# When the first latent tiles are normalised, and where layer 1's modulation is emitted, in a two-layer diffusion trunk on one core

## The chip, the cores and the metric

The kernel runs on one core of one Trainium2 chip. Its time is the device time of one execution in microseconds (us). A core has five engines that this text names: TensorE (PE in the profile; its weight loads are PEld), VectorE (DVE), ScalarE (ACT), GpSimd (POOL) and SyncE (SP), whose queue issues the DMAs. Each engine works through its own instructions in a fixed order.

## The reference

Two layers run over 1024 latent tokens and 256 context tokens of width 1024, in float32:

```python
for i in range(DEPTH):
    sh1, sc1, g1, sh2, sc2, g2 = modulation(c, w_ada[i], b_ada[i])         # silu(c) @ w_ada + b_ada, in six parts
    csh1, csc1, cg1, csh2, csc2, cg2 = modulation(c_ctx, w_ada[i], b_ada[i])
    h = modulate(rms_norm(x, norm1_g[i]), sh1, sc1)
    hc = modulate(rms_norm(ctx, norm1_g[i]), csh1, csc1)
    a_z, bq, bk, bv, cq, ck, cv = split_proj(h @ w_in[i])                  # and the same of hc
    ...
    x = x + g1 * (jnp.concatenate([out_a, out_b, out_c], axis=-1) @ w_out[i])
    x = x + g2 * conv_ffn(modulate(rms_norm(x, norm2_g[i]), sh2, sc2), w_up[i], conv_w[i], conv_b[i], w_down[i])
    # in layer 0 the context gets the same two updates
```

out_a is a chunked spatial gating, out_b a windowed attention with 8 heads, out_c a differential attention with 4 heads. conv_ffn is an up-projection to 2 x 2816 features, a convolution of width 3 over positions, silu(gate) * val, and a down-projection.

## The kernel before

**Arithmetic.** Every float32 operand is split in two parts, hi = round(x) and lo = x - hi, and a product is three matmuls (`mm3`). A weight unit (`wunit`) is one DMA into `raw` (three buffers, by SP), a rounding copy by ScalarE (L115) and a subtraction by VectorE or GpSimd (L109); its tile is `wsp` (three buffers). TensorE needs both parts.

**Order.** The program is written for a tile framework that schedules it: it simulates a time line of its own while the program is emitted, and from it decides the order of instructions on each engine. The order in which the code emits work is thus a hint, and what stands in which order is seen only in the resulting instruction lists.

**Start of layer 0.** Tokens are taken in tiles of 128: 0 to 7 are latent, 8 and 9 are context. `load_x` brings one tile from memory into `xin` (L336), transposes it on TensorE in two groups of four (L345), copies the result to `xc` (ScalarE L349, VectorE L347) and stores it to `x_s` in memory (L350). `norm_front` makes the mean square, GpSimd's power -0.5 (`nrs`, L211), a diagonal `dg` (L213), a broadcast by a matmul (L215) and the multiplication in place (L217); `norm_back` applies scale and shift (L225, L227), rounds to `h` (L228) and subtracts. `load_norm` is load_x and norm_front. Tiles 8, 9 and 0 went through load_norm ahead of the first projection; `norms` then finished the five tiles `al` = (8, 9, 0, 1, 2), and `ipset` projected all five with column blocks 3 and 2 of w_in (`inproj`; for each tile an `mm3` of 24 matmuls, L132, into `z`).

**Attention.** Until about 1100 us the attention of layer 0 runs, between and beside projections. `attn_c` ends each unit with a small chain: a reduction (`css`), VectorE's products, GpSimd's power -0.5 (`crs`, L748), VectorE's product (L749), the scaled output `o` (L751) and a transpose on TensorE (L755), whose result goes to memory (`o_s`) and from there, with the other heads, into the output projection (`oT` by L786).

**The MLP.** It runs over three groups of tokens (G0[0], G0[1], G0[2] in layer 0). Features are taken in steps f of 128, 22 in all, in blocks of 4, 4, 4, 4, 3, 3. A step has two halves (gate and value), each a w_up unit of 128 x 1024 (two halves' L115 rows are written `wsp 128x1024`) and 24 matmuls (L130). ScalarE (L847) and VectorE (L851, L854) do the convolution; L860, L861, L862, L864 and L109 make the gated product `g` in two parts. `down` takes a block's g with eight w_down units (128 x 512) of 12 matmuls each. Because five g buffers exist, down of the first block runs after five steps, the next after four more. While a group runs, `hook(f)` is called once in each step between its two halves, and puts other work there.

**Layer 1's modulation.** It is 12 column chunks of 512 (`ch`). `mod_wide` (L147 on) makes one chunk from four quarters of w_ada: a DMA of 512 KB into `mraw` (three buffers, L160), for each of its two k-slices and each stream a ScalarE scaling by the condition (the first into the accumulator `mev`, L166; the others into `mtr`, two buffers, L169), and for each `mtr` an add on GpSimd (L170). After the fourth quarter VectorE transposes and sums (L173, L174). Chunks 0 to 3, with both streams, ran in G0[1] at f = 0, 3, 6, 9; chunks 4 to 11, with one stream, in G0[2] at f = 0 to 7, a whole chunk in each call.

Of the kernel before, what the change touches and what calls it, by code (L numbers as in the profile page):

```python
# [25 lines left out]
AD = "mmmmd"  # L26
# [26 lines left out]
def trunk(ctx: ExitStack, tc: tile.TileContext, a: dict):  # L53
# [100 lines left out]
    def mod_wide(L, ch, ns, mkraw, mkacc, mktr):  # L154


        acc = [mkacc() for _ in range(ns)]
        for j in range(4):
            raw = mkraw()
            sp.dma_start(out=raw, in_=a["w_ada"][L, j * 256:j * 256 + 256, ch * 512:ch * 512 + 512]  # L160
                         .rearrange("(k p) c -> p k c", p=P))
            for k in range(2):
                for s in range(ns):
                    c1 = cpad[:, 2 * j + k, s:s + 1]
                    if j == 0 and k == 0:
                        act.activation(out=acc[s], in_=raw[:, k], func=AF.Identity, scale=c1)  # L166
                    else:
                        pr = mktr()
                        act.activation(out=pr, in_=raw[:, k], func=AF.Identity, scale=c1)  # L169
                        pool.tensor_tensor(out=acc[s], in0=acc[s], in1=pr, op=ALU.add)  # L170
        for s in range(ns):
            tr = mktr()
            dve.transpose(tr, acc[s])  # L173
            dve.tensor_reduce(out=st["modr"][:, :, ch, :, s].rearrange("p b m -> p m b"),  # L174
                              in_=tr.rearrange("p (m b j) -> p m b j", b=4, j=32), axis=AX.X, op=ALU.add)

# [154 lines left out]

    def load_x(i, wk, mkps):

        src = a["x"][0, i * P:i * P + P, :] if i < NLT else a["ctx"][0, (i - NLT) * P:(i - NLT) * P + P, :]
        xin = wk.tile([P, D], F32, tag="xin", name="xin")
        sp.dma_start(out=xin, in_=src)  # L336
        xc = wk.tile([P, KT, P], F32, tag="xc", name="xc", bufs=3)
        sq = wk.tile([P, D], F32, tag="nb", name="nb")
# [71 lines left out]

    def inproj(L, cb, tiles, hts, wk, wx, mkz, mkps, ws_=None):
        last = L == DEPTH - 1
        ws_ = ws_ or inproj_w(L, cb, wx)
        for i in tiles:
            kvonly = last and i >= NLT
            if kvonly and cb < 2:
# [579 lines left out]
    def modwide(L, ch, ns, p):  # L996
        mod_wide(L, ch, ns, lambda: p.tile([P, 2, 512], F32, tag="mraw", name="mraw", bufs=3),
                 lambda: p.tile([P, 512], F32, tag="mev", name="mev", bufs=2),
                 lambda: p.tile([P, 512], F32, tag="mtr", name="mtr", bufs=2))
# [8 lines left out]

    def load_norm(i):
        xc, ss = load_x(i, nwk, mkT)  # L1010
        norm_front(xc, mkT, None, xc, ss)
        return xc, "done"
# [4 lines left out]
    w3 = inproj_w(0, 3, wx)  # L1017
    pre.append(load_norm(0))
    ini.release()
# [3 lines left out]

    def ipset(L, tiles, cbs, wk_=None, wx_=None, w=None):
        for cb in cbs:
            wl = inproj(L, cb, tiles, hts, wk_ or wk, wx_ or wx, mkz, mkU, w)
            w = None
        return wl

    al, be = (8, 9, 0, 1, 2), (3, 4, 5, 6, 7)  # L1030
    norms(0, al, hts, hp, nwk, mkT, pre=pre, eng=NE[0], add=AD[0])
    setup2(ini2, 0, mkU)
    ipset(0, al, (3, 2), w=w3)
    setup3(ini2, 0, mkU)
# [58 lines left out]
    def hook(f):  # L1093
        ahead(0, G0[2], X3, f, HK[1], "x3")
        if f in (0, 3, 6, 9):
            modwide(1, f // 3, 2, ini)

# [15 lines left out]
    def hook(f):  # L1113
        if f < 8:
            modwide(1, 4 + f, 1, ini)
        if f == 3:
# [126 lines left out]
```

## Time and profile before

| | |
|---|---|
| time, median of 3 runs | 3356.69 us (3352.62 to 3362.18) |
| profiled execution | 3354.95 us |
| its span | 3353.1 us |
| granted TensorE clock, mean | 0.975 |
| DMA traffic | 499.52 MB, mean 149 GB/s |
| GpSimd's adds of the modulation, L170 | 112, 175.8 us, 1583 ns each |
| ScalarE's roundings of weights, L115 | 660, 555.9 us |
| VectorE's subtractions of weights, L109 | 516, 565.9 us |

The span is the time between the first and the last instruction of the profiled execution; the execution's time has a little around it. An engine's busy time is the sum of its instructions. In a table of stages, each row is a stretch (start:end), its length, then busy time and number of instructions for TensorE, its weight loads, VectorE, ScalarE and GpSimd, the granted TensorE clock, the DMA share and GB/s. In a timeline, each row has a start, a duration, the engine, the line and what it does, and in brackets the idle time before it and what ended that. In a table of groups, the two numbers behind the first bar are busy time in us and the mean of one in ns.

### The profile page before, as it was taken

How to read it: one execution, taken by the hardware profiler on the slowest of the kernel's cores; microseconds unless marked ns; L12 is line 12 of the kernel's file. 1: busy time of each engine (PE TensorE's matmuls, PEld its weight loads, DVE VectorE, ACT ScalarE, POOL GpSimd, SP SyncE). 2: the span in 40 equal slices, each digit the busy share in tenths (PEclk: the TensorE clock that was granted, in tenths of full speed). 3: DMA queues.
4: the chain of work that ended last, by engine and by line, in shares of the span. 5: the costliest groups of instructions: out<-in, count | busy, mean ns of one | idle time of the engine just before them, and what ended most of it. 6: DMA issues, size and time to landing. Idle time of an engine off the chain costs nothing. (4 is left out here: it accounts for less than half of the span.)

```text
span 3353.1 us, 54588 instructions
## 1 busy us (share of the span) xinstructions
PE 3164.3 (94%) x19503; PEld 2753.6 (82%) x19503; DVE 2342.6 (70%) x5306; ACT 1744.9 (52%) x3059; POOL 883.6 (26%) x1170
## 2 busy tenths in 40 slices
PE   6999998999999899999999899999999989999999
PEld 3777556887888798989999777666887779999998
DVE  5776756756878785878677678647786685666666
ACT  3555546555555653646444345556665564454443
POOL 1545211222233550128001154222322323222000
PEclk8999999999999999999999899999999999999999
DMA  8655777344542853378243556445645446434433
GB/s 259 194 156 162 223 248 186 89 121 124 136 116 83 255 154 110 103 207 242 87 117 112 160 149 161 126 139 136 167 135 149 122 118 189 120 111 135 137 114 108
DMA packets 754127, 499.52 MB, mean 149 GB/s; under 512 B 81480, under 2 KB 697792, under 8 KB 753856
## 3 DMA queue, kind: packets, MB, share of 16 engines
q1 hardware_dynamic: 753856, 496.03, 51.7%
q8 instruction: 155, 2.54, 0.3%
q14 instruction: 116, 0.95, 0.1%
HBM read 432.48 MB, written 63.44 MB: 148 GB/s over the span
## 5 line engine op out<-in xcount | busy, mean ns | idle before, releaser
L130 PE MATMUL z<-h,wsp 128*128 128x386 f32 (+3 forms) x5280 | 871.7, 318 | 20.4 <-DVE t L854 10.2
L130 PEld LDWEIGHTS z<-h,wsp 128*128 128x128 f32 x5280 | 822.0, 190 | 36.4 <-issue 13.9
L115 ACT ACTIVATE wsp<-raw 128x1024 fp32r<-128x1024 f32 (+2 forms) x660 | 555.9, 845 | 442.1 <-PE z L130 179.0
L109 DVE TENSOR_TENSOR wsp<-raw,wsp 128x1024 fp32r<-128x1024 f32 (+2 forms) x516 | 565.9, 1099 | 121.3 <-ACT wsp L115 118.5
L130 PE MATMUL z<-g,wsp 128*128 128x386 f32 (+3 forms) x2640 | 463.5, 323 | 17.8 <-ACT wsp L115 5.7
L130 PEld LDWEIGHTS z<-g,wsp 128*128 128x128 f32 x2640 | 418.1, 192 | 35.8 <-issue 11.0
L132 PE MATMUL z<-wsp,h 128*128 128x512 f32 x1584 | 404.8, 402 | 13.0 <-ACT wsp L115 3.3
L109 POOL TENSOR_TENSOR wsp<-raw,wsp 128x128 fp32r<-128x128 f32 x528 | 253.9, 513 | 448.8 <-ACT wsp L115 397.2
L132 PEld LDWEIGHTS z<-wsp,h 128*128 128x128 f32 x1584 | 291.6, 191 | 79.9 <-ACT wsp L115 4.3
L130 PE MATMUL zS<-h,wsp 128*128 128x386 f32 (+1 forms) x2112 | 333.7, 313 | 8.1 <-DVE t L854 3.2
L130 PEld LDWEIGHTS zS<-h,wsp 128*128 128x128 f32 x2112 | 318.9, 190 | 10.9 <-ACT wsp L115 4.3
L847 ACT ACTIVATE t<-z,cw 128x386 f32<-128x386 f32 (+3 forms) x220 | 137.8, 627 | 209.8 <-PE z L130 208.6
L851 DVE SCALAR_TENSOR_TENSOR t<-z,cw,t 128x255 f32<-128x255 f32 (+3 forms) x264 | 132.5, 502 | 144.6 <-ACT t L847 144.2
L682 ACT ACTIVATE ec<-ec,nmc 128x1280 f32<-128x1280 f32 (+1 forms) x144 | 182.1, 1265 | 52.1 <-DVE ec L483 51.0
L170 POOL TENSOR_TENSOR mev<-mev,mtr 128x512 f32<-128x512 f32 x112 | 175.8, 1583 | 124.6 <-ACT mtr L169 121.7
L130 PE MATMUL z<-oT,wsp 128*128 128x384 f32 (+2 forms) x1056 | 200.0, 336 | 4.9 <-DMA oT<-o_s 3.4
L130 PE MATMUL zS<-g,wsp 128*128 128x386 f32 (+1 forms) x1056 | 184.4, 319 | 14.9 <-ACT wsp L115 4.3
L483 DVE TENSOR_SCALAR_CACHE_REDUCE ec<-S,nmc 128x512 f32<-128x512 f32 (+1 forms) x256 | 156.7, 612 | 56.0 <-PE S L679 52.7
L879 DVE SCALAR_TENSOR_TENSOR xg<-z,mods,xg 128x384 f32<-128x384 f32 (+5 forms) x288 | 140.4, 501 | 75.8 <-PE z L130 74.7
L130 PEld LDWEIGHTS z<-oT,wsp 128*128 128x128 f32 x1056 | 176.1, 188 | 15.1 <-issue 4.9
L370 POOL TENSOR_TENSOR rs<-ss,cst 128x8 f32<-128x8 f32 (+1 forms) x76 | 119.5, 1572 | 259.5 <-DVE ss L368 187.7
L579 POOL TENSOR_SCALAR dgb<-cst,ls 128x128 f32<-128x128 f32 x144 | 89.2, 632 | 372.7 <-PE T L616 182.3
(248 smaller groups left out, 4848.1 us busy)
## 6 DMA issues: line engine op xcount, KB each, us to landing
raw<-in_w_up_dram SPq DMA_DIRECT2D x264, 512.0 KB
mraw<-in_w_ada_dram SPq DMA_DIRECT2D x96, 512.0 KB
raw<-in_w_down_dram SPq DMA_DIRECT2D x192, 256.0 KB
Kc<-qk_s SPq DMA_DIRECT2D x96, 320.0 KB
raw<-in_w_in_dram SPq DMA_DIRECT2D x52, 512.0 KB
raw<-in_w_out_dram SPq DMA_DIRECT2D x48, 512.0 KB
raw<-in_w_down_dram SPq DMA_DIRECT2D x104, 192.0 KB
qk_s<-st SPq DMA_DIRECT2D x18, 512.0 KB
```

What stands on the lines that cost most here:

```text
L109: eng.tensor_tensor(out=lo, in0=src, in1=hi.bitcast(F32), op=ALU.subtract)
L115: act.activation(out=hl[:, 0], in_=raw, func=AF.Copy)
L130: pe.matmul(ps, w(i, k), h(j, k), start=s, stop=e)
L132: pe.matmul(ps, h(i, k), w(j, k), start=s, stop=e)
L170: pool.tensor_tensor(out=acc[s], in0=acc[s], in1=pr, op=ALU.add)
L370: pool.tensor_tensor(out=rs[:, :ns], in0=ss[:, 1, :ns], in1=mhalf[:, :ns], op=ALU.pow)
L483: dve.tensor_scalar(out=neg, in0=s_ap, scalar1=-1.0, scalar2=init, op0=ALU.mult, op1=ALU.min, accum_out=acc)
L579: pool.tensor_scalar(out=dgs[ti][:, j], in0=ident, scalar1=ls[:, j:j + 1], scalar2=None, op0=ALU.mult)
L682: act.activation(out=e[:, :nk], in_=e[:, :nk], func=AF.Exp, scale=-1.0, bias=acc, accum_out=l1[:, m, ti:ti + 1])
L847: act.activation(out=t[:, o:o + n], in_=ps[:, :n], func=AF.Identity, scale=cw[:, L, 1, ft:ft + 1], bias=cw[:, L, 3, ft:ft + 1])
L851: dve.scalar_tensor_tensor(out=t[:, o + b + 1:o + e], in0=ps[:, b:e - 1], scalar=cw[:, L, 0, ft:ft + 1], in1=t[:, o + b + 1:o + e], op0=AL ...
L879: dve.scalar_tensor_tensor(out=xs, in0=ps[:, b + o0:b + o1], scalar=mods[:, L, 40 + ct, s:s + 1], in1=xs, op0=ALU.mult, op1=ALU.add)
```

## The change

It has two parts. In the first, tiles 0 and 1 are only fetched ahead of the first projection (`fetch_x`), norms finishes tiles 8 and 9, and a function `between` is called before each tile is projected with column block 3: it loads and normalises the tile that stands two places further in `al`. Column block 2 follows in a call of its own. In the second, `mod_wide` returns a function `quarter(j)`. In G0[1], one quarter is emitted in each of the steps 0 to 15; in G0[2], the 32 quarters are emitted over steps 0 to 13, two or three in each. The number of instructions on each engine stays the same.

```diff
--- before.py
+++ after.py
@@ -155,7 +155,8 @@
 
 
         acc = [mkacc() for _ in range(ns)]
-        for j in range(4):
+
+        def quarter(j):
             raw = mkraw()
             sp.dma_start(out=raw, in_=a["w_ada"][L, j * 256:j * 256 + 256, ch * 512:ch * 512 + 512]
                          .rearrange("(k p) c -> p k c", p=P))
@@ -168,11 +169,15 @@
                         pr = mktr()
                         act.activation(out=pr, in_=raw[:, k], func=AF.Identity, scale=c1)
                         pool.tensor_tensor(out=acc[s], in0=acc[s], in1=pr, op=ALU.add)
-        for s in range(ns):
-            tr = mktr()
-            dve.transpose(tr, acc[s])
-            dve.tensor_reduce(out=st["modr"][:, :, ch, :, s].rearrange("p b m -> p m b"),
-                              in_=tr.rearrange("p (m b j) -> p m b j", b=4, j=32), axis=AX.X, op=ALU.add)
+            if j < 3:
+                return
+            for s in range(ns):
+                tr = mktr()
+                dve.transpose(tr, acc[s])
+                dve.tensor_reduce(out=st["modr"][:, :, ch, :, s].rearrange("p b m -> p m b"),
+                                  in_=tr.rearrange("p (m b j) -> p m b j", b=4, j=32), axis=AX.X, op=ALU.add)
+
+        return quarter
 
     def mod_sum(L, c0, c1, ns, mkps):
 
@@ -329,11 +334,15 @@
         dve.tensor_scalar(out=cw[:, L, :, NFF:], in0=cw[:, L, :, NFF:], scalar1=0.5, scalar2=None, op0=ALU.mult)
 
 
-    def load_x(i, wk, mkps):
-
+    def fetch_x(i, wk):
         src = a["x"][0, i * P:i * P + P, :] if i < NLT else a["ctx"][0, (i - NLT) * P:(i - NLT) * P + P, :]
         xin = wk.tile([P, D], F32, tag="xin", name="xin")
         sp.dma_start(out=xin, in_=src)
+        return xin
+
+    def load_x(i, wk, mkps, xin=None):
+
+        xin = fetch_x(i, wk) if xin is None else xin
         xc = wk.tile([P, KT, P], F32, tag="xc", name="xc", bufs=3)
         sq = wk.tile([P, D], F32, tag="nb", name="nb")
         ss = sm.tile([P, 1], F32, tag="xss", name="xss")
@@ -408,10 +417,12 @@
         return [wunit(a["w_in"][L, u * 256:u * 256 + 256, cb * 512:cb * 512 + 512], 2, 512, wx if u == 3 else ws,
                       eng=E_[WD[st["wd"]][u]]) for u in range(4)]
 
-    def inproj(L, cb, tiles, hts, wk, wx, mkz, mkps, ws_=None):
+    def inproj(L, cb, tiles, hts, wk, wx, mkz, mkps, ws_=None, between=None):
         last = L == DEPTH - 1
         ws_ = ws_ or inproj_w(L, cb, wx)
         for i in tiles:
+            if between:
+                between(i)
             kvonly = last and i >= NLT
             if kvonly and cb < 2:
                 continue
@@ -994,7 +1005,7 @@
     setup_c(ini, mkU)
 
     def modwide(L, ch, ns, p):
-        mod_wide(L, ch, ns, lambda: p.tile([P, 2, 512], F32, tag="mraw", name="mraw", bufs=3),
+        return mod_wide(L, ch, ns, lambda: p.tile([P, 2, 512], F32, tag="mraw", name="mraw", bufs=3),
                  lambda: p.tile([P, 512], F32, tag="mev", name="mev", bufs=2),
                  lambda: p.tile([P, 512], F32, tag="mtr", name="mtr", bufs=2))
 
@@ -1006,8 +1017,8 @@
     modset(0, (2,), ini, "mev", ini, "mraw", 16, mkz, mkU)
     setup(ini, mkU)
 
-    def load_norm(i):
-        xc, ss = load_x(i, nwk, mkT)
+    def load_norm(i, xin=None):
+        xc, ss = load_x(i, nwk, mkT, xin)
         norm_front(xc, mkT, None, xc, ss)
         return xc, "done"
 
@@ -1015,22 +1026,31 @@
     modset(0, (3, 0, 1), ini, "mev", ini, "mraw", 16, mkz, mkU)
     mod_scale(0, 0)
     w3 = inproj_w(0, 3, wx)
-    pre.append(load_norm(0))
+    xins = [fetch_x(i, nwk) for i in (0, 1)]
     ini.release()
     hp = mkpool("h0", 8, "right")
     wk = mkpool("wk0", 2, "right")
     hts = {}
 
-    def ipset(L, tiles, cbs, wk_=None, wx_=None, w=None):
+    def ipset(L, tiles, cbs, wk_=None, wx_=None, w=None, between=None):
         for cb in cbs:
-            wl = inproj(L, cb, tiles, hts, wk_ or wk, wx_ or wx, mkz, mkU, w)
+            wl = inproj(L, cb, tiles, hts, wk_ or wk, wx_ or wx, mkz, mkU, w, between)
             w = None
         return wl
 
     al, be = (8, 9, 0, 1, 2), (3, 4, 5, 6, 7)
-    norms(0, al, hts, hp, nwk, mkT, pre=pre, eng=NE[0], add=AD[0])
+    norms(0, al[:2], hts, hp, nwk, mkT, pre=pre, eng=NE[0], add=AD[0])
+
+    def between(i):
+
+        n = al.index(i) + 2
+        if n < len(al):
+            j = al[n]
+            norms(0, (j,), hts, hp, nwk, mkT, pre=[load_norm(j, xins.pop(0) if xins else None)], eng=NE[0], add=AD[0])
+
     setup2(ini2, 0, mkU)
-    ipset(0, al, (3, 2), w=w3)
+    ipset(0, al, (3,), w=w3, between=between)
+    ipset(0, al, (2,))
     setup3(ini2, 0, mkU)
     norms(0, be, hts, hp, nwk, mkT, eng=NE[1], add=AD[1])
     ini2.release()
@@ -1092,8 +1112,10 @@
 
     def hook(f):
         ahead(0, G0[2], X3, f, HK[1], "x3")
-        if f in (0, 3, 6, 9):
-            modwide(1, f // 3, 2, ini)
+        if f < 16:
+            if f % 4 == 0:
+                st["q"] = modwide(1, f // 4, 2, ini)
+            st["q"](f % 4)
 
     wide(True)
     mlp(0, G0[1], *st["x2"], M, hook)
@@ -1111,8 +1133,10 @@
     al, be = (8, 9, 0, 1), (2, 3, 4, 5, 6, 7)
 
     def hook(f):
-        if f < 8:
-            modwide(1, 4 + f, 1, ini)
+        for n in range(32 * f // 14, 32 * (f + 1) // 14 if f < 14 else 0):
+            if n % 4 == 0:
+                st["q"] = modwide(1, 4 + n // 4, 1, ini)
+            st["q"](n % 4)
         if f == 3:
             setup2(ini, 1, mkT)
             setup3(ini, 1, mkT)
```

What the scheduler makes of it is shown at three places; the number behind a name in the first of them is the buffer's.

The first place is the start of layer 0, on TensorE: the rows around the projection of tile 0 (`z_651`), before. h_439 is tile 0's, xin_420 is tile 2, dg_455 and dg_475 belong to the norms of tiles 1 and 2.

```order
L132 MATMUL z_600<-wsp_341,h_409 128x512 x5
L345 MATMUL T_426<-cst_69,xin_420 128x128 x4
L345 MATMUL T_432<-cst_69,xin_420 128x128 x4
L215 MATMUL T_457<-dg_455,cst_69 128x128
L215 MATMUL T_477<-dg_475,cst_69 128x128
L132 MATMUL z_651<-wsp_326,h_439 128x512 x2
L345 MATMUL T_1176<-cst_69,xin_1170 128x128 x4
L132 MATMUL z_651<-wsp_326,h_439 128x512 x4
```

The same place with the change, where h_461 is tile 0's, xin_611 is tile 2, and dg_544 and dg_634 belong to tiles 1 and 2:

```order
L132 MATMUL z_561<-wsp_341,h_366 128x512 x5
L220 MATMUL T_546<-dg_544,cst_69 128x128
L354 MATMUL T_617<-cst_69,xin_611 128x128 x4
L354 MATMUL T_623<-cst_69,xin_611 128x128 x4
L132 MATMUL z_651<-wsp_326,h_461 128x512 x2
L220 MATMUL T_636<-dg_634,cst_69 128x128
L354 MATMUL T_1176<-cst_69,xin_1170 128x128 x4
L132 MATMUL z_651<-wsp_326,h_461 128x512 x4
```

The broadcast of tile 1 has moved ahead of the transposes of tile 2, and that of tile 2 behind the first two matmuls of tile 0's projection.

The second place is the end of layer 0's attention in G0[1], on GpSimd. The last crs row is that of the last unit of attn_c. Before:

```order
L748 TENSOR_TENSOR crs<-css,cst 128x2
L109 TENSOR_TENSOR wsp<-raw,wsp 128x128 x12
L170 TENSOR_TENSOR mev<-mev,mtr 128x512 x7
L748 TENSOR_TENSOR crs<-css,cst 128x2
L170 TENSOR_TENSOR mev<-mev,mtr 128x512 x49
```

With the change:

```order
L109 TENSOR_TENSOR wsp<-raw,wsp 128x128 x21
L759 TENSOR_TENSOR crs<-css,cst 128x2
L109 TENSOR_TENSOR wsp<-raw,wsp 128x128 x15
L759 TENSOR_TENSOR crs<-css,cst 128x2
L171 TENSOR_TENSOR mev<-mev,mtr 128x512 x56
```

The last crs stood behind seven of the 56 adds of this group; now it stands ahead of all of them.

The third place is the first down block of G0[1], on ScalarE, from its second w_down unit (`wsp 128x512`) on. Before, up to the fourth:

```order
L115 ACTIVATE wsp<-raw 128x512
L864 ACTIVATE g<-t 128x386
L169 ACTIVATE mtr<-mraw,cpad 128x512 x2
L860 ACTIVATE th<-t 128x386
L169 ACTIVATE mtr<-mraw,cpad 128x512
L847 ACTIVATE t<-z,cw 128x386
L169 ACTIVATE mtr<-mraw,cpad 128x512 x2
L864 ACTIVATE g<-t 128x386
L169 ACTIVATE mtr<-mraw,cpad 128x512
L115 ACTIVATE wsp<-raw 128x512
L169 ACTIVATE mtr<-mraw,cpad 128x512 x2
L115 ACTIVATE wsp<-raw 128x512
```

With the change, from the second unit to the seventh:

```order
L115 ACTIVATE wsp<-raw 128x512
L170 ACTIVATE mtr<-mraw,cpad 128x512
L875 ACTIVATE g<-t 128x386
L115 ACTIVATE wsp<-raw 128x512
L170 ACTIVATE mtr<-mraw,cpad 128x512 x2
L115 ACTIVATE wsp<-raw 128x512
L170 ACTIVATE mtr<-mraw,cpad 128x512 x2
L115 ACTIVATE wsp<-raw 128x512
L170 ACTIVATE mtr<-mraw,cpad 128x512
L115 ACTIVATE wsp<-raw 128x512 x2
```

Between the second and the third w_down unit six scalings stood, and now one stands there. On SP's queue, the loads of the x tiles for the output projection (`xg`), seven of which stood between the third and the fifth w_down load, now all stand ahead of the second.

## The prediction

> **What bounds the kernel now.** The page's busy table comes first.
>
> ```profile
> span 3353.1 us, 54588 instructions
> PE 3164.3 (94%) x19503; PEld 2753.6 (82%) x19503; DVE 2342.6 (70%) x5306; ACT 1744.9 (52%) x3059; POOL 883.6 (26%) x1170
> ```
>
> TensorE is busy for 94%, and the order lists as many matmuls after the change as before, so the change can only win what TensorE idles or is slowed where pieces move. The second view is therefore a table of stages over the second MLP group, where the first pieces of layer 1's modulation run, with two quiet stretches, the third MLP group and the worst stretch of the attention behind them.
>
> ```profile
> core 0: us, PE busy (x) PEld busy (x) DVE busy (x) ACT busy (x) POOL busy (x), PEclk, DMA share, GB/s
> 1110.14:1150.86 40.72, 36.74 (x195) 36.41 (x195) 36.40 (x47) 30.67 (x52) 29.01 (x19) 0.92 0.68 218
> 1150.86:1178.55 27.69, 20.29 (x98) 18.04 (x97) 21.20 (x26) 18.28 (x30) 23.22 (x17) 0.94 0.91 292
> 1178.55:1214.01 35.46, 34.21 (x193) 33.89 (x193) 32.67 (x34) 27.09 (x40) 32.62 (x19) 1.00 0.57 168
> 1214.01:1238.29 24.28, 20.55 (x97) 19.25 (x97) 19.32 (x29) 10.03 (x16) 4.73 (x4) 0.86 0.42 124
> 1240.00:1260.00 20.00, 20.00 (x116) 20.00 (x115) 13.14 (x19) 8.94 (x13) 0.00 (x0) 1.00 0.43 122
> 1460.00:1600.00 140.00, 128.69 (x1053) 126.72 (x1052) 119.90 (x169) 89.48 (x143) 98.29 (x65) 1.00 0.80 230
> 1640.00:1660.00 20.00, 20.00 (x169) 20.00 (x168) 14.00 (x24) 9.36 (x14) 0.00 (x0) 1.00 0.23 66
> 550.00:600.00 50.00, 37.68 (x183) 26.07 (x183) 41.93 (x111) 34.80 (x65) 8.95 (x7) 0.76 0.55 137
> ```
>
> The row 1240 to 1260 gives the full rate: 20 us / 116 = 0.1724 us a matmul. The first four rows are up 1 (eight half-steps of 24 matmuls), down 1 (eight w_down units of 12), up 2 and down 2. 192 matmuls need 33.1 us and 96 need 16.6, so these stretches lose 40.72 - 33.1 = **7.6**, 27.69 - 16.6 = **11.1**, 35.46 - 33.1 = **2.4** and 24.28 - 16.6 = **7.7 us**, 28.8 in all. VectorE is busy for 36.40 + 21.20 + 32.67 + 19.32 = 109.6 of their 128.15 us, so they can't shrink by more than 18.6 unless VectorE's own work gets shorter.
>
> TensorE's timeline says where these losses lie.
>
> ```profile
> 1131.12 0.45 PE L755 MATMUL T<-cst,o 128*128 128x128 f32 x1 [3.98 <-DVE o L751]
> 1131.69 6.64 PE L130 MATMUL zS<-h,wsp 128*128 128x386 f32 x24
> 1142.39 4.40 PE L130 MATMUL zS<-h,wsp 128*128 128x386 f32 x24
> ...
> 1158.82 0.62 PE L130 MATMUL zS<-g,wsp 128*128 128x386 f32 x2 [3.55 <-ACT wsp L115]
> 1160.37 3.46 PE L130 MATMUL zS<-g,wsp 128*128 128x386 f32 x10 [0.92 <-DVE wsp L109]
> 1165.89 2.04 PE L130 MATMUL z<-g,wsp 128*128 128x386 f32 x10 [1.59 <-DVE wsp L109]
> ...
> 1180.41 4.13 PE L130 MATMUL zS<-h,wsp 128*128 128x386 f32 x22 [1.25 <-DVE wsp L109]
> ...
> 1223.30 3.58 PE L130 MATMUL zS<-g,wsp 128*128 128x386 f32 x10 [2.87 <-DVE wsp L109]
> ```
>
> Up 1 loses 3.98 us to one transpose of the last attention unit, and 6.64 - 4.40 = 2.2 us to the slow half-step behind it. Down 1 waits for weight splits. What ScalarE, GpSimd and VectorE do ahead of those two releases:
>
> ```profile
> 1121.28 3.29 POOL L170 TENSOR_TENSOR mev<-mev,mtr 128x512 f32<-128x512 f32 x2 [0.42 <-ACT mtr L169]
> 1124.68 0.94 POOL L748 TENSOR_TENSOR crs<-css,cst 128x2 f32<-128x2 f32 x1
> 1129.43 1.22 DVE L749 TENSOR_TENSOR crs<-crs,rl 128x2 f32<-128x2 f32 x1
> 1130.69 0.29 DVE L751 TENSOR_TENSOR o<-oq,crs 128x128 f32<-128x128 f32 x1
> ...
> 1147.40 0.62 ACT L115 ACTIVATE wsp<-raw 128x512 fp32r<-128x512 f32 x1
> 1155.47 0.72 ACT L169 ACTIVATE mtr<-mraw,cpad 128x512 f32<-128x512 f32 x1 [0.84 <-POOL mev L170]
> 1158.16 0.61 ACT L115 ACTIVATE wsp<-raw 128x512 fp32r<-128x512 f32 x1
> ```
>
> GpSimd takes the unit's crs behind the modulation's adds, VectorE follows with work in between, and TensorE's transpose is the end of that chain. ScalarE's second and third w_down split stand 10.8 us apart, and between them it waits for GpSimd to free the two mtr buffers.
>
> Last, VectorE in 100 us with adds (1120 to 1220, first five rows; the GpSimd window tells how many) and in 100 us without (1240 to 1340, the last four).
>
> ```profile
> L109 DVE TENSOR_TENSOR wsp<-raw,wsp 128x1024 fp32r<-128x1024 f32 x13 | 22.2, 1716 | 1.4 <-ACT wsp L115 1.4
> L109 DVE TENSOR_TENSOR wsp<-raw,wsp 128x512 fp32r<-128x512 f32 x10 | 11.8, 1194 | 0.0
> L861 DVE SCALAR_TENSOR_TENSOR th<-th,t 128x386 f32<-128x386 f32 x8 | 9.6, 1202 | 0.8 <-ACT th L860 0.8
> L109 DVE TENSOR_TENSOR g<-t,g 128x386 fp32r<-128x386 f32 x7 | 8.3, 1182 | 0.7 <-ACT g L864 0.6
> L854 DVE SCALAR_TENSOR_TENSOR t<-zS,cw,t 128x385 f32<-128x385 f32 x8 | 4.9, 608 | 0.1
> ...
> 1120.00:1220.00 100.00, 81.53 (x52) 0.95 0.68 215
> ...
> L109 DVE TENSOR_TENSOR wsp<-raw,wsp 128x1024 fp32r<-128x1024 f32 x18 | 22.0, 1222 | 5.1 <-ACT wsp L115 5.1
> L109 DVE TENSOR_TENSOR wsp<-raw,wsp 128x512 fp32r<-128x512 f32 x8 | 5.5, 687 | 0.2
> L861 DVE SCALAR_TENSOR_TENSOR th<-th,t 128x386 f32<-128x386 f32 x5 | 2.8, 555 | 0.7 <-ACT th L860 0.7
> L854 DVE SCALAR_TENSOR_TENSOR t<-zS,cw,t 128x385 f32<-128x385 f32 x5 | 3.1, 619 | 0.1
> ```
>
> Beside GpSimd's adds, VectorE's operations on two SBUF operands are longer: 13 x 0.494 + 10 x 0.507 + 8 x 0.647 + 7 x 0.627 (g, against the 555 ns of th, which has its size) = 21.1 us. Operations that read PSUM are not (608 against 619 ns). Over 52 adds that is **0.41 us of VectorE for each add**.
>
> **The change, part by part.** *Start of layer 0.* Nothing is removed: the norms of tiles 0, 1 and 2 are emitted between tile projections. The rows of SP's queue, the two early fetches among them, stand in the same order through the start, so no load is moved past another. On TensorE the order shows one move: tile 1's broadcast now stands ahead of tile 2's transposes. Tile 0's projection is still behind both.
>
> ```profile
> 69.97 1.22 DVE L217 TENSOR_TENSOR xc<-xc,T 128x1024 f32<-128x1024 f32 x1 [0.20 <-DMA x_s<-xc]
> 70.58 1.22 PE L132 MATMUL z<-wsp,h 128*128 128x512 f32 x2 [2.04 <-ACT h L228]
> 72.72 6.42 PE L132 MATMUL z<-wsp,h 128*128 128x512 f32 x22
> ```
>
> That projection waits for ScalarE's h and then VectorE's, and the in-place multiply before them for a store to land; these pieces are the same. I take **0**. The bounds are one wait and one multiply each way, 2.04 + 1.22 = 3.3: -3 to +3.
>
> *Second MLP group.* The 56 scalings and 56 adds stay (4 chunks, 2 streams, 7 each). The program emits one quarter per step to f = 15, but the order shows ScalarE still taking all of them by about the middle, since the scheduler places what is ready. By ScalarE's order, up 1, down 1, up 2 and down 2 hold 15, 17, 19 and 5 adds before, and 16, 11, 16 and 13 after.
>
> Up 1: in GpSimd's order the last crs now stands ahead of every add, and its transpose follows 58 instead of 143 matmuls of this group, with 42 others (7.2 us) between it and the unit's previous one; the chain needs 0.94 + 1.22 + 0.29 us and VectorE's rows between. So the 3.98 us go, and with them the 2.2 behind, less 0.6 for a wait of the chain that may stay: **-5.6**, bounds 0 (another wait takes its place) and -7.6.
>
> Down 1: before, six scalings stand between the second and the third split; after, at most two stand between any neighbours, and the wait of 3.55 goes. Six adds fewer free 6 x 0.41 = 2.5 us of VectorE, of which I count three quarters, VectorE being busy for 21.20 of 27.69 us: 1.9. **-5.5**, bounds 0 and -11.1. SP's order helps here: before, loads of x tiles stand between w_down loads; after, nearly all of them stand ahead of these.
>
> Up 2: 3 adds fewer, 1.2 us, three quarters of it: **-0.9**, bounds 0 and -2.4. Down 2: 8 adds more, 3.3 us, three quarters: **+2.5**. Bounds: with few adds it already has a wait of 2.87 us, which may go (-2.9), and the full 3.3 with 0.5 for a longer split (+3.8).
>
> *Third group.* The quarters are spread over 14 steps where eight whole chunks were, but the order of TensorE is the same row for row, and so are the scalings on ScalarE and the reductions on VectorE. This stretch does lose time beside its adds: at the 169 matmuls per 20 us of the later stretch without adds, 1053 need 124.6 of 140 us, so 15.4 go. With the same order I count **0** of it; that a different moment of issue on SP helps or hurts is covered by the bounds below.
>
> *Attention, 190 to 1100 us.* No line of it is changed, but the scheduler deals its projection matmuls otherwise among the attention's short ones. The longest runs without such filler are 333, 213, 67 and 115 matmuls before and 292, 232 and 115 after: no better or worse by this. **0**, with 50 - 37.68 = 12.3 us, what the worst stretch idles now, as the bound each way.
>
> Sum: -5.6 - 5.5 - 0.9 + 2.5 = **-9.5 us**. The profiled execution took 3354.95 us, 1.85 around its span, and the median is 1.74 above it. 3354.95 - 9.5 = 3345.5 by its clock, and on the scale of the median **3347**.
>
> [...]
>
> **The rivals.** *B, VectorE's floor.* If the split chain flows throughout, the four stretches shrink to VectorE's 109.6 us: -18.6, 3338 on the median's scale. For it: the waits in down 1 come in a chain from one pile-up. Against: down 2 loses 7.7 us with 4 adds.
>
> *C, the change doesn't do what it says, or contention only moves.* The scheduler pulls the quarters ahead in both versions. If each add's 0.41 us hits TensorE wherever it stands and the crs chain waits for something else, the sum is 0: 3357 (3353 to 3359). For it: 56 adds stay, and 109.6 of 128.15 us of VectorE. Against: the waits of 3.98 and 3.55 have places in the order that are gone.
>
> *D, slower: the rearranged attention runs short of filler.*
>
> ```profile
> PE S L679 <- DVE ec L483: 12.3, 17, 2.9
> ```
>
> This is the largest wait of TensorE there: scores wait for the softmax to free their bank. One more stretch as thin as 550 to 600 costs 12.3 us: 3356.7 + 12.3 = 3369 with no gain, 3359.5 with the gain of 9.5; it decides above that gain. Against it: the longest runs without filler are no longer.
>
> **How the numbers follow.** A, the forecast (3341 to 3352): 0.40. B (3333 to 3341): 0.18. C: 0.22. D (3359 to 3371): 0.20. About 0.3%, 10 us, is what a measurement of this kernel can tell from no change: faster below 3346.6, slower above 3366.8. Half of A and all of B are faster: 0.38. The other half of A, C and two fifths of D are within: 0.50. The rest of D, three fifths because more than one stretch of the attention could thin: 0.12. The range 3333 to 3364 takes in A, B, C and D's near end, some 0.85; A alone has 3341 to 3352.
>
> **What would show it.** Right: no wait for o at the last transpose of the attention, up 1 near 35 us; no split gap of 10 us on ScalarE, down 1 near 22; down 2 near 27; the third group and the start unchanged within 3 us. Wrong: down 1 still near 27 (C), the four stretches near 110 (B), or more than 5 us lost between 190 and 1100 us (D).

## The result, and the profile after

| | before | with the change |
|---|---|---|
| median | 3354.65 us (4 runs) | 3334.28 us (4 runs, 3331.55 to 3337.91) |
| ratio, 95% interval | | 0.9936, 0.9916 to 0.9957 |
| the same again, more runs | 3353.57 us (15 runs) | 3334.70 us (5 runs); 0.9951, 0.9938 to 0.9963 |
| profiled execution, its span | 3354.95, 3353.1 us | 3336.65, 3334.8 us |

By the medians the kernel is 19 to 20 us faster; the two intervals run from 12 to 28 us. The table of stages of the kernel with the change shows the four stretches of the prediction (up 1, down 1, up 2, down 2 of the second MLP group); the columns are those of the prediction's table.

```profile
core 0: us, PE busy (x) PEld busy (x) DVE busy (x) ACT busy (x) POOL busy (x), PEclk, DMA share, GB/s
1104.92:1143.87 38.95, 35.16 (x195) 33.53 (x194) 32.30 (x39) 27.36 (x43) 26.07 (x16) 1.00 0.93 316
1143.87:1168.97 25.10, 20.55 (x97) 19.58 (x97) 19.30 (x26) 16.45 (x26) 17.28 (x12) 0.86 0.67 200
1168.97:1202.84 33.87, 33.87 (x194) 33.87 (x193) 29.38 (x36) 26.59 (x41) 29.51 (x18) 1.00 0.66 193
1202.84:1224.61 21.77, 18.10 (x98) 16.80 (x98) 21.74 (x27) 13.16 (x21) 17.08 (x11) 1.00 0.41 119
```

They take 119.7 us where they took 128.15: -1.8, -2.6, -1.6 and -2.5. TensorE's idle time in them (length less PE busy) falls from 16.4 to 12.0 us; in up 1 it hardly falls, from 3.98 to 3.79. The timeline shows why.

```profile
1106.69 0.27 PE L766 MATMUL T<-cst,o 128*128 128x128 f32 x1
1132.13 4.15 PE L130 MATMUL zS<-h,wsp 128*128 128x386 f32 x22 [0.97 <-DVE wsp L109]
1138.63 4.15 PE L130 MATMUL z<-h,wsp 128*128 128x386 f32 x22 [1.64 <-DVE wsp L109]
1143.87 0.62 PE L130 MATMUL zS<-g,wsp 128*128 128x386 f32 x2 [1.08 <-ACT wsp L115]
1148.42 0.63 PE L130 MATMUL z<-g,wsp 128*128 128x386 f32 x2 [1.31 <-ACT wsp L115]
1151.69 3.59 PE L130 MATMUL z<-g,wsp 128*128 128x386 f32 x10 [2.65 <-DVE wsp L109]
```

The last transpose of the attention no longer waits (3.98 us before) and stands 24 us earlier. TensorE then reaches the last weight splits of up 1 and the first of down 1 before they are ready, and up 1 ends with three waits for them (0.97, 1.64 and 1.08 us) that it didn't have before. In down 1 (the last two rows) it still waits for splits, only less.

The next table has the larger stretches, of the kernel before and then of the kernel with the change. Its rows are: the second MLP group from its first w_up matmul to the first matmul of its third down block; the rest of that group; the third group up to its 960th w_up matmul; and the end of layer 1's attention, from the first w_out matmul of layer 1's second MLP group until 288 of that group's w_up matmuls are done.

```profile
1096.48:1272.16 175.68, 159.31 (x864) 153.17 (x865) 138.95 (x173) 107.13 (x166) 89.57 (x57) 0.95 0.63 193
1272.16:1457.78 185.62, 183.94 (x982) 172.57 (x981) 124.70 (x195) 85.01 (x135) 12.60 (x8) 1.00 0.41 118
1457.78:1637.10 179.32, 165.75 (x1358) 163.03 (x1359) 147.23 (x217) 102.72 (x161) 98.29 (x65) 1.00 0.73 210
2567.16:2801.89 234.73, 218.24 (x1384) 184.54 (x1383) 153.25 (x376) 125.81 (x227) 61.06 (x105) 0.96 0.47 124
```

```profile
1096.34:1259.33 162.99, 150.38 (x819) 146.12 (x819) 133.75 (x172) 104.12 (x161) 90.63 (x57) 0.98 0.65 202
1259.33:1444.60 185.27, 183.86 (x982) 172.58 (x981) 124.68 (x195) 85.15 (x135) 12.58 (x8) 1.00 0.41 117
1444.60:1624.28 179.68, 167.23 (x1357) 164.49 (x1358) 144.50 (x217) 102.89 (x161) 98.25 (x65) 0.99 0.73 210
2557.38:2784.31 226.93, 211.97 (x1361) 182.15 (x1360) 150.98 (x371) 124.03 (x223) 61.17 (x105) 0.97 0.46 124
```

Up to the second group nothing changes (1096.5 and 1096.3 us), and neither does the rest of that group (-0.35) or the third (+0.4). **The second group gains 12.7 us, and layer 1's attention, which the change doesn't touch, 7.8 us.** A second profile of the changed kernel gives the same two, 162.0 and 226.6 us. The stretch between the third and the fourth row seems to give back 3.0 (930.1 to 933.1 us), but it takes 930.6 in that second profile; what follows gains 0.7, for -18.3 in the span. Of the 12.7 us, 8.9 are TensorE's busy time and 3.8 its idle time; in layer 1 it is 6.3 of 7.8. Matmuls have gone from both rows: in the second group 45 (x864 to x819), the last units of layer 0's attention, which now stand ahead of it, and in layer 1's 23 (x1384 to x1361), which stand before and behind it now.

### The profile page after: what moved, and what is told of

The parts are those of the page before. It is cut to its first block, busy times and chain, and to the rows that moved or that the text cites. A ratio compares the mean times of both kernels' runs of the same rounds, so it can differ in the third digit from the quotient of the medians.

```text
span 3334.8 us, 54592 instructions
## 1 busy us (share of the span) xinstructions
PE 3154.3 (95%) x19503; PEld 2751.2 (82%) x19503; DVE 2336.3 (70%) x5306; ACT 1746.6 (52%) x3059; POOL 889.1 (27%) x1170
## 4 chain that ended last, share of the span: by engine, by line
PE 72%; DVE 9%; DMA 5%; ACT 3%; issue 2%; POOL 2%; SPq 1%; ACTq 0%; POOLq 0%; DVEq 0%
PE z L130 35%; PE zS L130 12%; PE z L132 7%; PE O L716 3%; PE O L617 3%; PE T L607 2%; PE T L725 2%; DVE wsp L109 2%; PE S L690 2%; PE zS L132 1%; DVE ec L494 1%; DMA mraw<-in_w_ada_dram 1%; POOL mev L171 1%; DVE ec L700 1%; ACT wsp L115 1%
```

## The experiments

The instruction lists say more than was read in them for the prediction. With the second part of the change alone, the orders of TensorE, VectorE, ScalarE and SyncE are those of before, row for row, and GpSimd's but for one swap in the third group: on the old start, it makes no difference to the scheduler where the code emits the modulation. So the last crs can have moved only by the first part. With the first part in place, though, the quarters of the second group do alter the order from its first down block on; why there and not on the old start wasn't looked into. Four theories could be told apart: the start's new order carries all (A); the quarters do (B); two separate rearrangements do, one in each place (C); and an earlier start does.

**The parts alone.** The first part alone, with whole chunks in both hooks:

```diff
-        if f < 16:
-            if f % 4 == 0:
-                st["q"] = modwide(1, f // 4, 2, ini)
-            st["q"](f % 4)
+        if f in (0, 3, 6, 9):
+            q = modwide(1, f // 3, 2, ini)
+            for j in range(4):
+                q(j)
...
```

> The change's first part alone (start of layer 0); the modulation is emitted in whole chunks as before. Theory A, the gain comes from the new deal of instructions that the start's allocations set off: 3328 to 3342 us, within 6 us of the changed kernel, and the stretch of the second MLP group up to its third down block near 163 us (175.7 before). Theory B, the gain comes from the quarters: 3350 to 3360 us, that stretch near 176 us.

Measured: 0.9993 (0.9982 to 1.0004). The second part alone (quarters in both hooks, the start as before):

> The change's second part alone (quarters in both MLP groups); the start is as before. Its instructions stand in the same order as before on TensorE, VectorE and ScalarE. Theory A: 3352 to 3358 us, no difference, second MLP group 175.7 us, last transpose of the attention waits about 4 us as before. Theory B: 3330 to 3345 us, second group below 168 us.

Measured: 0.9997 (0.9988 to 1.0005). Both parts alone do nothing that the total can tell, so neither A nor B is the whole: the first kernel's 3349.96 us is all but in B's range, the second's 3352.43 in A's. The stages tell more. Each kernel's row of the second group and of layer 1's attention end, first part alone (in its second set of runs, below), then second part alone:

```profile
1098.63:1263.55 164.92, 152.32 (x819) 147.52 (x819) 134.56 (x172) 103.81 (x159) 91.08 (x57) 0.97 0.65 199
2555.11:2791.36 236.25, 218.53 (x1383) 184.57 (x1382) 152.62 (x376) 125.78 (x227) 61.31 (x105) 0.96 0.46 124
```

```profile
1098.84:1272.35 173.51, 159.26 (x864) 152.79 (x865) 138.81 (x173) 107.43 (x166) 89.82 (x57) 0.95 0.63 194
2566.14:2800.47 234.33, 217.54 (x1383) 184.43 (x1382) 152.65 (x376) 125.80 (x227) 61.22 (x105) 0.96 0.46 125
```

The first part brings the second group to 164.9 us and leaves layer 1 at 236.3 (163.5 and 235.2 in its first set); the second part alone changes neither. That kernel has the order of before, so it also shows what one execution is worth: 173.5 against 175.7 for the group, 37.7 and 29.7 against 40.7 and 27.7 for its up 1 and down 1, a wait of 1.89 us against 3.98 at the last transpose of the attention. A stage of 30 to 180 us is known to some 2 or 3 us; the first 1100 us, in profiles whose rows there are the same, only to some 5.

**Two other starts.** Both are the first part with a smaller edit, `xins = []` (no early fetch) and `for i in (0,)` (one early fetch).

> First part without the early fetches of tiles 0 and 1 (they are loaded between the projections), modulation in whole chunks. In GpSimd's order the last crs stands behind 10 adds. Theory A (another deal; the crs behind adds costs up 1 some 4 to 6 us): second MLP group 172 to 178 us, total anywhere from 3335 to 3370 us. Rival, the early start of layer 0 itself carries the gain: start longer by 2 to 5 us and the second group near 163 us.

> First part with only tile 0 fetched early, modulation in whole chunks. In GpSimd's order the last crs stands behind 7 adds, as before the change. Theory A: second MLP group 172 to 178 us, total anywhere from 3335 to 3370 us. Rival, normalising the tiles between projections carries the gain whatever the deal: 3330 to 3342 us.

Measured: 1.0014 (1.0005 to 1.0023) and 0.9989 (0.9978 to 1.0000). In the first, the second group takes 179.4 us (172 to 178 was expected) and layer 1's end 233.0; in the second 174.8 and 227.7:

```profile
1100.77:1275.57 174.80, 158.12 (x865) 151.09 (x865) 138.41 (x173) 107.24 (x166) 88.59 (x57) 0.96 0.63 194
2566.20:2793.85 227.65, 212.58 (x1372) 181.42 (x1371) 149.83 (x373) 126.19 (x226) 62.06 (x105) 0.97 0.46 125
```

All tiles are normalised between projections in both, and neither gains what the change gains: an early start of layer 0 is not it. The two gains also come singly: the first part alone has the short second group without the short end of layer 1, one early fetch has the reverse. By the profiles that is theory C, two gains; the totals of these two kernels fall by less than their stages (see the end of the next section).

**The changed kernel again, and half of its quarters.** The kernel as it is, and the same with whole chunks in the third group only:

> The changed kernel as it is, beside the kernel before in more rounds. Theory C (two new deals, the second MLP group with the last crs ahead of the adds, -12 us, and the attention's end in layer 1, -8 us): ratio 0.992 to 0.996. Rival (part of the first figure is scatter between runs, and the real gain is one deal at most): 0.996 to 0.999.

> Both parts, but in the third MLP group whole chunks at f = 0 to 7 as before. On TensorE, VectorE, ScalarE and SyncE the order is that of the changed kernel. If the quarters matter only in the second group (and only on top of the first part): ratio 0.994 to 0.9965, as the changed kernel. If the third group's quarters carry a part: above 0.997.

> The first part alone once more, on the same chip as the kernel above, which differs from it by the quarters of the second group. If its second group's gain of 12 us shows up in the total: ratio 0.9955 to 0.998. If, as in its first runs, most of that is lost elsewhere: 0.998 to 1.000, and its profile shows the part up to the second group 3 to 5 us longer than in the changed kernel again.

Measured: 0.9951 (0.9938 to 0.9963), 0.9953 (0.9940 to 0.9967) and, for the first part alone, 0.9989 (0.9979 to 1.0000). The quarters of the third group do nothing, as its order said. The second and third of these kernels ran on the same chip and differ by the quarters of the second group: 3336.89 against 3348.43 us, 11.5 us. Of these, the profiles show 9.8 in layer 1's end:

```profile
1096.89:1260.12 163.23, 150.38 (x820) 146.19 (x820) 132.06 (x172) 103.52 (x159) 90.57 (x57) 0.98 0.65 202
2551.62:2778.04 226.42, 211.56 (x1361) 181.77 (x1360) 150.85 (x371) 123.94 (x223) 61.07 (x105) 0.97 0.46 125
```

So the quarters are worth what they are by moving layer 1's attention, 1300 us behind the place where they stand. This doesn't hang on one profile: layer 1's end takes 226.4 to 226.9 us in the three profiles with the second group's quarters on the new start, and 234.3 to 236.3 in five others (the kernel before, the second part alone, the first part alone twice, and the kernel of the next experiment). The first part's profile was expected to be 3 to 5 us longer up to the second group; this time it was 1.7.

**What holds the second group up.** Kernel before, with the last crs made to stand ahead of the adds:

```diff
+                if L == 0 and hd == 3 and tuple(tiles) == (6, 7):
+                    dve.tensor_scalar(out=z0, in0=rs[:, 0:1], scalar1=0.0, scalar2=None, op0=ALU.mult)
+                    dve.tensor_scalar(out=cp2, in0=cpad, scalar1=z0, scalar2=None, op0=ALU.add)
...
-                    c1 = cpad[:, 2 * j + k, s:s + 1]
+                    c1 = (cp2 if ns == 2 else cpad)[:, 2 * j + k, s:s + 1]
```

> Kernel before with one thing added: the modulation's scalings in the second MLP group read a copy of the condition that VectorE makes behind the last crs of layer 0 (two small VectorE operations more), so all 56 adds stand behind that crs on GpSimd; the rest of the start and of the attention stays as before. If the crs behind the adds is what costs the second group: that stretch 161 to 167 us instead of 175.7, ratio 0.995 to 0.9985 (layer 1's end stays as before, 234 us). If the gain there comes from something else in the new deal: stretch 172 to 178 us, ratio 0.999 to 1.001.

Measured: 0.9987 (0.9978 to 0.9996), the second group 167.1 us; the group lies at the edge of the first band, 161 to 167, and the ratio between the two bands. GpSimd's timeline, and the transpose on TensorE:

```profile
1112.58 0.69 POOL L750 TENSOR_TENSOR crs<-css,cst 128x2 f32<-128x2 f32 x1 [22.14 <-DVE css L747]
1117.37 2.55 POOL L172 TENSOR_TENSOR mev<-mev,mtr 128x512 f32<-128x512 f32 x2 [4.09 <-ACT mtr L171]
...
1119.96 0.27 PE L760 MATMUL T<-cst,o 128*128 128x128 f32 x1
```

```profile
1093.62:1260.76 167.14, 155.88 (x865) 150.33 (x866) 136.07 (x175) 107.52 (x166) 90.31 (x57) 0.97 0.65 201
```

The crs comes 12 us earlier than before (9 when counted from the group's first matmul), no transpose waits, and the group is 6.4 us shorter than with the second part alone, 8.5 shorter than before, with all 865 matmuls still in it. Nearly all of it is in up 1: 34.2 us, against 40.7 before and 37.7 with the second part alone; down 1, at 27.8 us, is no shorter. The edit also holds back the modulation's scalings until the crs is done, and the scheduler orders the group and parts of layer 1 anew around it, so it shows what the place of the crs is worth together with that. With the crs behind 10 adds (no early fetch) the transpose waited 3.62 us and the group took 179.4; behind 7, in three profiles, 1.9 to 4.0 and 173.5 to 175.7; ahead of them, nothing and 162 to 167. From this kernel to the changed one it is another 4 us: TensorE's busy time is 5.5 us less there, with 45 matmuls fewer in the row, and its idle time 1.35 more.

Next, the adds themselves are left out, in the kernel before and in the changed one (`if ns == 1:` ahead of the add). Without them the scheduler also orders the rest anew, so each difference is the price of the adds together with the order that they bring. Each kernel ran once, in 3336.57 and 3326.23 us:

> Kernel before without GpSimd's adds in the second MLP group (layer 1's modulation of chunks 0 to 3 is then incomplete); ScalarE's scalings stay. If the adds cost this stretch by the longer VectorE operations and the wait for crs: 152 to 160 us instead of 175.7, VectorE's w_up subtractions there about 1220 ns instead of 1716. If ScalarE's scalings and the loads are what costs: 170 us or more.

> Changed kernel without the same adds. If the adds' cost is the same wherever they stand, apart from the crs: 152 to 160 us as in the other one, against 163.0 with adds.

```profile
1097.77:1259.57 161.80, 153.69 (x865) 148.35 (x865) 110.50 (x173) 104.83 (x166) 0.70 (x1) 0.99 0.68 210
```

```profile
1097.92:1252.26 154.34, 149.37 (x820) 146.53 (x819) 109.37 (x172) 101.12 (x159) 0.70 (x1) 0.98 0.70 213
```

The 56 adds cost the group 175.7 - 161.8 = 13.9 us in the order of before, and 163.0 - 154.3 = 8.7 in that of the change. VectorE's busy time falls by 138.95 - 110.50 = 28.5 and 133.75 - 109.37 = 24.4 us, and in the kernel before its w_up subtractions take 1219 ns between 1120 and 1220 us, where they took 1716. My band for the kernel before, 152 to 160, was missed by 1.8: without adds its group is still 7.5 us longer than the other's. Of these, 4.3 are TensorE's busy time, with 45 matmuls of the attention's end still in the row.

**The spreading, enforced.** How many scalings into `mtr` (those that an add follows, 56 in all) ScalarE takes between one g and the next in the second group, by the instruction lists:

```
before          5 5 4 4 5 22 4 5 2
with the change 5 3 5 3 4 17 5 4 5 5
enforced        2 3 4 5 2 4 4 3 3 4 4 3 3 4 4 2 2
```

The change spreads the quarters in the code over 16 steps; the scheduler takes them in 10, with a pile in the first down block as before. The third line is a kernel in which each quarter's scalings depend on the g of the step before (`st["g"]`, set in the second group alone or in both):

```diff
         def quarter(j):
+            cp = cpad[:, 2 * j:2 * j + 2]
+            if st.get("g") is not None:
+                nq[0] += 1
+                cp = cq[:, nq[0] % 4]
+                dve.tensor_scalar(out=z0, in0=st["g"][:, 0, 0:1].bitcast(F32), scalar1=0.0, scalar2=None, op0=ALU.mult)
+                dve.tensor_scalar(out=cp, in0=cpad[:, 2 * j:2 * j + 2, 0:2], scalar1=z0, scalar2=None,
+                                  op0=ALU.add)
...
-                    c1 = cpad[:, 2 * j + k, s:s + 1]
+                    c1 = cp[:, k, s:s + 1]
```

> Changed kernel with the spreading enforced in the second group: each quarter's scalings read a small copy of the condition that VectorE makes behind the g of the step before (32 tiny VectorE operations more), so ScalarE takes 2 to 5 scalings a step to f = 16, with no pile of 17 in the first down block. If piled adds cost that stretch (154.3 us without adds, 163 with): 155 to 159 us, the stretch behind it at most 2 us longer, total 2 to 8 us below the changed kernel, ratio 0.992 to 0.9945. If an add costs TensorE the same wherever it stands: the first stretch shorter, the one behind it longer by as much, ratio 0.9945 to 0.997.

> The same in the third group too, to f = 13. That group loses about 15 us of TensorE in its first 140 us. If that is the piled adds: the group 4 to 10 us shorter, ratio 0.989 to 0.993. If adds cost the same anywhere, or the third group's loss has another cause: no further gain against the run above.

Measured: 0.9963 (0.9951 to 0.9975) in the second group alone, 0.9943 (0.9931 to 0.9955) in both. The rows of the first of the two: second group, the rest of it, third group to its middle.

```profile
1100.67:1254.45 153.78, 147.49 (x820) 146.13 (x819) 125.44 (x189) 94.14 (x146) 66.90 (x43) 0.98 0.68 207
1254.45:1448.80 194.35, 187.66 (x982) 175.44 (x981) 136.69 (x209) 94.00 (x152) 32.62 (x22) 0.98 0.40 118
1448.80:1629.78 180.98, 168.33 (x1358) 165.95 (x1358) 143.15 (x217) 102.76 (x161) 97.14 (x65) 0.98 0.72 208
```

The second group is as short as without adds (153.8 us), 9.2 shorter than with the change, and the rest of it, where 14 adds have gone (x22 against x8), is 194.35 - 185.27 = 9.1 longer. Nothing is won, as the second of the two expectations had it. VectorE is busy for only 137 of 194 us there. TensorE waits 6.7 us in that stretch where it waited 1.4; the first two rows are its largest waits, the third VectorE's w_down subtractions in 100 us around them (1280 to 1380):

```profile
PE zS L133 <- DVE wsp L112: 2.2, 1, 2.2
PE z L133 <- DVE wsp L112: 2.1, 1, 2.1
...
L112 DVE TENSOR_TENSOR wsp<-raw,wsp 128x512 fp32r<-128x512 f32 x8 | 5.4, 679 | 0.0
```

The subtractions that TensorE waits for aren't longer than without adds (679 against 687 ns). They come late because other work stands ahead of them in VectorE's order between 1352 and 1366 us: a `th` of 1.65 us beside the last adds, a `t` of 2.02 beside a subtraction on GpSimd, transposes and reductions of the modulation, and pieces of the third group's norms. What each of these costs was not separated, and 3.8 of the 9.1 us are TensorE's busy time. With the third group enforced too, that group up to its 960th w_up matmul:

```profile
1448.45:1621.05 172.60, 164.25 (x1352) 162.60 (x1352) 143.04 (x258) 94.05 (x147) 70.75 (x47) 1.00 0.70 199
```

Here spreading pays, as expected for the group though not for the total: 172.6 against 179.7 us, and 178 to 181 in every other profile; the rest of that group isn't longer (261.5 against 262.8 us from there to the same matmul of layer 1's first projection). Yet the total is that of the changed kernel (3333.85 against 3334.28 to 3336.89 us): both kernels have other rearrangements in layer 1, the stretch from there to layer 1's attention end takes 937.7 us here against 933.1, and the stretch up to the second group is 4 us longer in both, on rows that are those of the changed kernel, which is within what such profiles differ by. No version beats the change by more than the runs can tell.

## Why the prediction came out as it did

The measured time lies in the range, near its lower end; 3347 was 13 us too long. That it lies in the range at all is partly luck: the four stretches that were worked out give 8.5 of the 18.3 us, and by other mechanisms than forecast; the rest came from places that the sum put at 0. Of the signs that the prediction named for being right, up 1 near 35 us, down 1 near 22 and down 2 near 27 did not come (38.95, 25.10 and 21.77).

- *Start:* 0 was forecast, and the rows up to the second group end at 1096.3 against 1096.5 us. Right.
- *Layer 0's attention:* 0 was forecast. It is a little longer up to the first MLP group, whose first w_up matmul stands at 602.0 to 604.1 us in the four profiles with the old order there and at 605.2 to 610.5 in the eight with the new one. The first MLP group then makes up for part of it, with 490.3 to 492.2 us where it took 491.6 to 494.8.
- *Up 1:* -5.6 forecast, -1.8 measured, and -0.7 when the two profiles with the order of before (40.7 and 37.7) are set against the three with that of the change (37.7 to 38.95). The wait of 3.98 us did go, and the place of the crs was its cause: with the crs put first, up 1 took 34.2 us, about what was forecast. But in the changed kernel TensorE came to the next weight splits earlier and waited there. The bound of 0 named this ("another wait takes its place"); the value took the gain in full. The wait was also read from one execution: with the same order another had 1.89.
- *Down 1:* -5.5 forecast, -2.6 measured, -3.9 over the same five profiles. The wait of 3.55 us went, and waits of 1.31 and 2.65 stand in its place.
- *Up 2, down 2:* -0.9 and +2.5 forecast, -1.6 and -2.5 measured (-1.4 and -1.8 over the five). The step that failed is to count three quarters of VectorE's added time as time of the stretch. In down 2 VectorE's time did rise as forecast, by 21.74 - 19.32 = 2.4 us with 11 adds where there were 4, but it had 24.28 - 19.32 = 5.0 us to spare, and the stretch became shorter. TensorE's idle time hardly changed (3.73 and 3.67 us); its busy time fell from 20.55 to 18.10 us, with a granted clock of 0.86 before and 1.00 after. What lowered the clock there wasn't tried.
- *The price of an add:* 0.41 us of VectorE was too low, since it left out one operation on two SBUF operands, `t<-t,th`. Its rows in the same two windows of the kernel before, with adds and without:

```profile
L862 DVE TENSOR_TENSOR t<-t,th 128x386 f32<-128x386 f32 x7 | 8.0, 1136 | 0.1
L862 DVE TENSOR_TENSOR t<-t,th 128x386 f32<-128x386 f32 x4 | 2.2, 557 | 0.0
```

  With 7 x 0.579 = 4.1 us more it is 25.1 us, 0.48 for each add. In the changed kernel's 100 us with 50 adds (1110 to 1210), the w_up subtractions are hardly longer, others more:

```profile
L109 DVE TENSOR_TENSOR wsp<-raw,wsp 128x1024 fp32r<-128x1024 f32 x14 | 17.7, 1265 | 0.0
L109 DVE TENSOR_TENSOR wsp<-raw,wsp 128x512 fp32r<-128x512 f32 x11 | 12.0, 1094 | 0.3 <-ACT wsp L115 0.3
L872 DVE SCALAR_TENSOR_TENSOR th<-th,t 128x386 f32<-128x386 f32 x8 | 10.9, 1363 | 0.3 <-ACT th L871 0.2
L873 DVE TENSOR_TENSOR t<-t,th 128x386 f32<-128x386 f32 x8 | 10.7, 1332 | 0.1
L109 DVE TENSOR_TENSOR g<-t,g 128x386 fp32r<-128x386 f32 x8 | 7.6, 944 | 2.2 <-ACT g L875 2.2
```

  With the quiet durations that is 14 x 0.043 + 11 x 0.407 + 8 x 0.808 + 8 x 0.775 + 8 x 0.389 = 20.9 us, 0.42 for each add. The kernels without adds give 28.5 / 56 = 0.51 and 24.4 / 56 = 0.44. So VectorE's price changes little with the order, though which operations bear it changes a lot; TensorE's price is 13.9 / 56 = 0.25 and 8.7 / 56 = 0.16. The Trainium skill (page "SBUF — State Buffer", section "SBUF: two separate sides") says that VectorE and GpSimd share a port pair under an exclusive lock, which VectorE meets in a 2-port mode, or with two SBUF inputs beside a GpSimd operation that reads SBUF. The trace agrees with the second case: the rows above are longer, and those that read PSUM, at 605 to 614 ns, are not. That an add costs about the same of VectorE's time in any stretch was my inference, and these two orders bear it out roughly; that TensorE loses three quarters of it was another, and by these figures it loses a third to a half.
- *The sum* of the four stretches, -9.5, is close to the -8.5 measured because these errors cancel. 128.15 us did not approach VectorE's floor: the time lies in rival B's range, its mechanism was not met.
- *What was left out:* the first feature step ahead of up 1, which gained 5.1 us (13.66 us from 1096.48 to 1110.14, 8.58 from 1096.34 to 1104.92) since the attention's last matmuls no longer stand in it, and **layer 1's attention, 7.8 us**. The prediction saw that the attention was rearranged, bounded that at 12.3 us each way, and put 0; it looked only at layer 0. The bound held, and the place did not.
- *Which part does it:* the text on the second group spoke of the quarters as if they made its new order. The place of the crs and the matmuls that left the group come from the start; the quarters change the order from the first down block on, and layer 1's attention. The prediction compared only the order before with that of both parts together, so it could not tell.
- *Third group:* 0 forecast, +0.4 measured. Right.
- *Rival C* (the scheduler pulls the quarters ahead) was right in what it said of the scheduler and wrong in its time; *rival D*, less filler in the attention, went the other way in the total.

Two things stay open. The first is that single gains reach the total only in part. The first part alone has the second group shorter by 9 to 12 us in its profiles, and its medians are 3.4 us lower (3349.96 and 3348.43 against 3352.12 and 3353.11, the kernel before in the same sets). Early fetch of one tile has layer 1's end 7.1 us shorter and a median 2.7 lower; the crs put first has the group 6.4 to 8.5 shorter and a median 4.3 lower. The profiled executions show more: those of the first part (3347.55 and 3343.19 us) lie 8.4 below those of the two kernels with the order of before (3354.95 and 3352.57). But its 23 executions run from 3342.8 to 3359.1 us, so a few profiled ones can lie this far from the median by chance, and what the new order loses up to the second group (that stretch takes 1098.6 us in the mean of the eight profiles, 1096.7 in the four) takes a small part. The changed kernel's own 19 to 20 us, and the 11.5 us that the second group's quarters are worth on the new start, are totals and don't hang on this. The second is what makes layer 1's attention shorter in one order than in the other: fewer matmuls stand in that stretch (1361 against 1384), its waits are about as long (15.0 and 16.5 us idle), and the stretches ahead of it and behind it are not longer than profiles of one order differ by. It wasn't tried.

## What to carry to other kernels

Where a scheduler decides the order, moving code may change nothing, or it may rearrange work 2000 us later: here the same quarters did the first on one start and the second on another. Compare the orders for each part of a change alone, and on top of the other part, before giving a gain to one of them. A wait that is removed is worth what the next wait leaves of it, so take the full amount only where the stretch behind it has slack. What GpSimd's work adds to VectorE's time is not simply time of the stretch: in one place 2.4 us more of it came with a shorter stretch, in another VectorE was busy for 137 of 194 us and TensorE waited for it all the same. And read a wait from more than one execution: with one order, the wait that carried the forecast was 3.98 us in one and 1.89 in the other.

## What the runs showed that was not expected

Two parts that each do nothing that their totals can tell (0.9993 and 0.9997) gave 0.5 to 0.6% together: on the old start the quarters leave the orders of TensorE, VectorE, ScalarE and SyncE as they are, and on the new one they rearrange layer 1's attention. And 56 adds of 1.6 us on GpSimd, an engine that is busy for a quarter of the span, cost TensorE 13.9 us in one order and 8.7 in the other: by longer operations on VectorE, by a late crs and by ScalarE's waits for mtr buffers, whose shares were not separated beyond the crs.
